# Five places for weight blocks and longer runs of paired slabs in a streamed MLP layer

## The chip, the cores and the metric

The kernel runs on one core of a Trainium2 chip. The metric is the device time of one execution in microseconds, the median of several runs. The profile comes from a single further execution, so its own time stands beside the median below.

## The reference

One encoder layer on a sequence of 256 tokens of width 2048, all in float32. Three residual branches follow one another: a mix of four token mixers, a cross attention, and a gated MLP; a norm ends it. The change touches the MLP and what feeds its weights.

```python
def swiglu(h, w_gate_up, w_down):
    gate, up = jnp.split(h @ w_gate_up, 2, axis=-1)
    return (jax.nn.silu(gate) * up) @ w_down
...
        x = x + mix @ w_out[l]
        x = x + cross_attention(rms_norm(x, norm_g[l, 1]), mem_n, w_xq[l], w_xkv[l], w_xo[l])
        x = x + swiglu(rms_norm(x, norm_g[l, 2]), w_gate_up[l], w_down[l])
    return rms_norm(x, final_norm_g)
```

w_gate_up is 2048 x 11264, w_down 5632 x 2048.

## The kernel before

**Arithmetic.** TensorE multiplies in a shorter format, fp32r. So each weight is used as a sum of two: `wh`, the weight cast to fp32r by ScalarE, and `wl`, the raw weight minus `wh`, subtracted by VectorE. Activations are kept in the same way as a high and a low half of one slot. `part` (L430) multiplies one activation tile of 128 tokens with 512 columns of weights in three matmuls: high x wh (L432), high x wl (L433), low x wh (L434).

**The stream of weights.** All weights of the layer come in one sequence of 252 slabs of 128 partitions x 2048 floats (16 blocks of 128 x 128). `Stream` (L72) loads and converts them. `_load` (L94) brings a slab into `raw` (three buffers) by a transfer on SP's queue. `_half` (L112) converts half a slab, 1024 columns: a cast at L135 and a subtraction at L136, into a *place*, a pair of tiles wh and wl. `_buffers` (L88) picks the place: three in the pool `wp`, and one in `extra`, a pool that exists in most of the kernel and takes every fourth block. `_fill` (L166) runs when TensorE's program takes a block: it writes down conversions until three blocks more than the one in use are made. So a block is converted into a place that TensorE has finished with, and the number of places sets how far the conversion runs ahead.

**Normal and paired slabs.** In w_gate_up and w_down a plan of letters says how each slab is used. In an N slab two halves of 1024 columns are multiplied with two tiles of 128 tokens: eight parts. In an S slab (`PAIRED`, L50) two tiles along the summed dimension, two groups of columns and the two tiles of tokens are multiplied as 2 x 2 blocks with seven products instead of eight (the Strassen-Winograd scheme). This needs sums of weight blocks, made from the raw slab, and sums of activations, made once by `combine` (L437) into tiles `z`. `_sums` (L140) hands out an S slab as four blocks of 1024, 512, 1024 and 1024 columns: two, one, two and two parts. Call s0, s1, s2 the first three quarters of the raw slab and s3 the last.

- block one (`ph` 0): s1 and s2 as loaded
- block two: s0 as loaded
- two adds on VectorE (L158): the tile `two` holds (s1 + s3, s2 + s3); the first add makes s1 := (s1 + s3) + s2, the second s2 := s1 + s0
- block three: `two`
- block four: s1 and s2, so it reads what the second add wrote

In w_gate_up (`SUMMED`, L52) the tile `two` is made by transfers: when the slab before an S slab is loaded, SP loads the last quarter of the S slab twice, into both halves of `two` (L101), and a transfer on POOL's queue adds the two middle quarters to it in memory (L102). The S slab's own raw load then brings three quarters only. `two` has two buffers of its own.

**The order of work.** The tile framework places the instructions of each engine at build time; `keep_place` (L308) pins a run of them behind the instruction before. Work that isn't part of the stream (norms, combinations, splitting of loaded activations) is written as generators in `Background` (L204), which is polled after each part and steps a generator when VectorE's counted backlog is under 0.9 us.

**The MLP.** Slabs 120 to 127 are the first columns of w_gate_up, by `gemm_rows` (L521); in this time the last features of the attention arrive (`ar`) and are put into the slots `h3`. Ten groups of eight slabs follow, slabs 128 to 207, by `paired_rows` (L463): each makes 512 gate and 512 up columns by the plan `GROUP`, "NNSNSNSN". In a group `mixed` (L1064) combines four of the seven products when the last S slab is done, and `gated` (L1073) applies the gate's nonlinearity after that when the gate's normal tiles are done, which by this plan is at the end of the last S slab (one N slab follows). `upped` and `up` multiply gate and up at the end of the group, and `store_turned` transposes the result and writes it to memory ("hidden"). `fetch` (L1087) loads it back and splits it into the slots `f` for w_down. The residual `res` (four tiles of 128 x 1024 floats) isn't used from the end of the attention until w_down. In w_down (slabs 208 to 251) the plans `PASSES` apply.

Of the kernel before, what the change touches and what calls it, by code (L numbers as in the profile page):

```python
# [13 lines left out]
F32 = mybir.dt.float32  # L14
F32R = mybir.dt.float32r
# [4 lines left out]
ALU = mybir.AluOpType  # L20
# [3 lines left out]
P = 128  # L24
# [25 lines left out]
PAIRED = {a + i for a, plan in [(GATE_UP + 8 * j, GROUP) for j in range(10)] + [(DOWN, PASSES[0]), (DOWN + 22, PASSES[1])]  # L50
          for i, x in enumerate(plan) if x == "S"}
SUMMED = {i for i in PAIRED if i < DOWN}  # L52

# [18 lines left out]
class Stream:  # L72


    def __init__(self, tc, pools, W, bg):
        self.tc, self.nc, self.W, self.bg = tc, tc.nc, W, bg
        self.rawp, self.wp = pools
        self.order = []
        self.n = self.made = 0
        self.after = []  # L80
        self.halves = []
        self.at = self.phase = 0
        self.raw = None
        self.extra = self.sums = None
        self.places = []
        self.two = []

    def _buffers(self, n, m):  # L88
# [165 lines left out]
class Block:  # L254
    def __init__(self, ctx, tc, t):
# [10 lines left out]
        self.st = Stream(tc, (rawp, wp), t["W"], self.bg)  # L266
        self.kept = itertools.count()
        self.run()

# [193 lines left out]
    def paired_rows(self, w, cols, slots, sums, plan, mixed, first, ready=None, late=0, before=None, swap=False):  # L463
# [23 lines left out]
        for i, kind in enumerate(plan):  # L487
            if before:
                before(i)
            if kind == "S":  # L490
                ks, z = next(todo)
# [75 lines left out]
    def run(self):  # L567
# [20 lines left out]
        self.ff = self.outside("hidden", FT)  # L588
        self.gk = [nc.dram_tensor(f"state{i}", (R, P), F32, kind="Internal").ap() for i in range(4)]
        self.vd = nc.dram_tensor("values", (P, 8 * 512), F32, kind="Internal").ap()  # L590
        def load(src, k, n):
# [16 lines left out]
        nc.scalar.copy(self.identr, self.ident)  # L608
        with self.tc.tile_pool(name="wx", bufs=1) as st.extra:
            self.attention(self.mixers())  # L610
# [256 lines left out]
    def attention(self, ps):  # L867
        tc, nc, act, st = self.tc, self.nc, self.act, self.st
        with tc.tile_pool(name="atp", bufs=1) as atp, tc.tile_pool(name="kp", bufs=1) as kp, \
# [110 lines left out]
            late.append(self.bg.add(self.arrive(self.xf[1], 2, self.tmp, self.put3, FAR), go=True))  # L980
            st.extra = None
            self.add_rows(1, 3, self.gemm_rows("w_xo", [1536], o)[0])
# [46 lines left out]
    def mlp(self):  # L1029
        tc, nc, act = self.tc, self.nc, self.act  # L1030
        with tc.tile_pool(name="fp", bufs=1) as fp:
            self.gap(fp, 192)
            f = [fp.tile([P, 512], F32R, name=f"f{i}") for i in range(14)]
            z = [fp.tile([P, 1024], F32R, name=f"z{i}") for i in range(3)]
            f = act[4:12] + f + [z[i // 2][:, i % 2 * 512:i % 2 * 512 + 512] for i in range(6)] + self.h3
            with tc.tile_pool(name="wy", bufs=1) as self.st.extra:
                self.gap(self.st.extra, 64)
                with tc.tile_pool(name="tw", bufs=2) as self.st.sums, tc.tile_pool(name="gp", bufs=1) as gp:
# [8 lines left out]
    def gate_up(self, gp, f, z):  # L1047
# [76 lines left out]
        comb = self.bg.add(combined())  # L1124
        ps = self.gemm_rows("w_gate_up", [0, DFF], self.h3,
                            parts=[(range(8), [0]), (range(8, 12), [0]), (range(12), [1]), (range(12, 16), [0]), (range(12, 16), [1])],
                            before=lambda n: n in (1, 3) and self.bg.drain(self.late if n == 1 else last))
        self.bg.drain(col)
# [4 lines left out]
        for j in range(1, DFF // 512):  # L1133
            upped(j, self.paired_rows("w_gate_up", [j * 512, DFF + j * 512], self.h3, sums, GROUP, mixed, gated, swap=j % 2 == 0)[0])
        self.bg.drain(early)
        self.fetch = self.bg.add(fetch(FT - 22, FT, 6, SOON))

    def down(self, f, sp):
# [54 lines left out]
        for i, plan in enumerate(PASSES):  # L1193
# [5 lines left out]
            def before(j):  # L1199
                while plan[j] == "S" and len(made) <= plan[:j].count("S"):  # L1200
                    self.bg.step(next(e for e in self.bg.q if e[0] is g))
                if late and j == len(plan) - 2:
                    st.extra = None

# [686 lines left out]
```

## Time and profile before

| what | us |
|---|---|
| median of three runs | 1437.49 (1437.12 to 1438.29) |
| the profiled execution's own time | 1434.72 |
| its span in the profile | 1432.9 |
| TensorE busy in it | 1423.0 |
| VectorE busy | 1145.7 |
| ScalarE busy | 815.8 |

Some 1.8 us of the profiled execution lie outside the span. Times in the views count from the span's start. A busy share is an average over the whole kernel; what a change in one part is worth is read from that part's own window. Matmuls overlap each other, so a matmul's own duration is longer than the pitch at which they follow one another. In the views L432 is line 432 of the kernel, `wl<-raw,wh` names the tiles written and read, and the name in brackets behind an idle time is what ended it.

### The profile page before, as it was taken

To read this page: it belongs to the slowest core of one execution; us is meant where nothing else is said; L and a number is where in the kernel's file an instruction comes from. 1 tells how busy PE (TensorE), PEld (TensorE's weight loads), DVE (VectorE), ACT (ScalarE), POOL (GpSimd) and SP (SyncE) were. 2 spreads that over 40 slices of the span, in tenths; PEclk is the share of its full clock that TensorE was granted. 3 is DMA by queue.
4 is the path that set the end of the run, shared out by engine and by line. 5 is a ranking of instruction groups with operands and counts; after the bars stand their busy time and mean duration, and the time that the engine had idled before them with its cause. 6 is when DMAs were issued, how large, how long until landed. Compare 5 with 4: busy or idle time off the path is not lost.

```text
span 1432.9 us, 18653 instructions
## 1 busy us (share of the span) xinstructions
PE 1423.0 (99%) x6589; PEld 1181.4 (82%) x6589; DVE 1145.7 (80%) x1738; ACT 815.8 (57%) x1183; POOL 234.6 (16%) x306
## 2 busy tenths in 40 slices
PE   9999999999999999999999999999999999999997
PEld 8888888888888888888888888888888888788886
DVE  6667868777877767777677888889888888989997
ACT  7556565446745555556455556555555556655655
POOL 0000100013212223531430121122011002000000
PEclk9999999999999999999999999999999999999999
DMA  9877554456667787865986989899999887665554
GB/s 350 299 291 247 205 202 166 171 172 224 198 199 232 235 271 246 275 201 171 287 242 207 283 280 289 275 275 285 294 293 289 264 265 227 217 231 180 193 219 147
DMA packets 73038, 343.80 MB, mean 240 GB/s; under 512 B 10957, under 2 KB 12654, under 8 KB 45168
## 3 DMA queue, kind: packets, MB, share of 16 engines
q1 hardware_dynamic: 54848, 288.98, 57.6%
q0 software_dynamic: 17664, 52.97, 15.6%
q8 instruction: 51, 0.84, 0.2%
q10 hardware_dynamic: 432, 0.66, 0.1%
q14 instruction: 43, 0.35, 0.1%
HBM read 322.12 MB, written 20.45 MB: 239 GB/s over the span
## 4 chain that ended last, share of the span: by engine, by line
PE 98%; DVE 1%; DMA 0%; ACT 0%; issue 0%; SPq 0%; ACTq 0%
PE pg L432 22%; PE pg L433 22%; PE pg L434 22%; PE pm L432 7%; PE pm L434 7%; PE pm L433 7%; PE pg L380 4%; PE pg L381 2%; PE pm L1344 1%; PE pm L1022 1%; PE pm L993 1%; PE pm L1753 0%; DMA raw<-in_W 0%; DVE res L282 0%; PE pm L994 0%; PE pm L1518 0%
## 5 line engine op out<-in xcount | busy, mean ns | idle before, releaser
L136 DVE TENSOR_TENSOR wl<-raw,wh 128x1024 fp32r<-128x1024 f32 (+1 forms) x413 | 494.1, 1211 | 167.6 <-ACT wh L135 164.8
L135 ACT CAST wh<-raw 128x1024 fp32r<-128x1024 f32 (+1 forms) x413 | 424.7, 1043 | 282.9 <-PE pg L434 188.3
L432 PE MATMUL pg<-wh,act 128*128 128x512 f32 (+1 forms) x1191 | 465.5, 391 | 0.0
L433 PE MATMUL pg<-wl,act 128*128 128x512 f32 (+1 forms) x1191 | 463.9, 389 | 0.1
L434 PE MATMUL pg<-wh,act 128*128 128x512 f32 (+1 forms) x1191 | 463.8, 390 | 0.0
L432 PEld LDWEIGHTS pg<-wh,act 128*128 128x128 f32 x1191 | 224.0, 188 | 47.9 <-issue 1.5
L434 PEld LDWEIGHTS pg<-wh,act 128*128 128x128 f32 x1191 | 223.9, 188 | 47.5 <-DVE act L282 0.6
L433 PEld LDWEIGHTS pg<-wl,act 128*128 128x128 f32 x1191 | 224.0, 188 | 46.5 <-DVE wl L136 1.2
L147 ACT CAST wh<-raw 128x1024 fp32r<-128x1024 f32 (+1 forms) x150 | 137.4, 921 | 149.6 <-PE pg L434 53.8
L148 DVE TENSOR_TENSOR wl<-raw,wh 128x1024 fp32r<-128x1024 f32 (+1 forms) x150 | 155.9, 1060 | 52.8 <-ACT wh L147 52.6
L433 PE MATMUL pm<-wl,act 128*128 128x512 f32 x309 | 120.3, 389 | 0.1
L432 PE MATMUL pm<-wh,act 128*128 128x512 f32 x309 | 120.2, 389 | 0.0
L434 PE MATMUL pm<-wh,act 128*128 128x512 f32 x309 | 120.2, 389 | 0.0
L380 PE MATMUL pg<-act,wh 128*128 128x512 f32 x256 | 90.5, 395 | 0.0
L381 PE MATMUL pg<-act,wl 128*128 128x256 f32 x256 | 71.8, 280 | 0.0
L433 PEld LDWEIGHTS pm<-wl,act 128*128 128x128 f32 x309 | 58.0, 188 | 12.3 <-DVE wl L136 0.4
L434 PEld LDWEIGHTS pm<-wh,act 128*128 128x128 f32 x309 | 58.0, 188 | 12.1
L432 PEld LDWEIGHTS pm<-wh,act 128*128 128x128 f32 x309 | 58.0, 188 | 12.0
L102 POOL DMA_DIRECT2D two<-in_W x30 | 26.6, 885 | 237.6 <-DMA two<-in_W 106.4
L158 DVE TENSOR_TENSOR raw<-raw 128x512 f32<-128x512 f32 x90 | 61.8, 687 | 1.2
L147 ACT CAST wh<-two 128x1024 fp32r<-128x1024 f32 x30 | 31.5, 1051 | 52.0 <-PE pg L434 27.0
L380 PEld LDWEIGHTS pg<-act,wh 128*128 128x128 f32 x256 | 48.1, 188 | 10.5
(375 smaller groups left out, 1819.3 us busy)
## 6 DMA issues: line engine op xcount, KB each, us to landing
raw<-in_W SPq DMA_DIRECT2D x216, 1024.0 KB, 5.6
raw<-in_W SPq DMA_DIRECT2D x30, 768.0 KB, 6.3
two<-in_W SPq DMA_DIRECT2D x60, 256.0 KB, 4.8
two<-in_W POOLq DMA_DIRECT2D x30, 512.0 KB, 9.0
raw<-in_W SPq DMA_DIRECT2D x11, 512.0 KB, 7.1
hidden<-g POOLq DMA_DIRECT2D x22, 256.0 KB, 3.8
tmp<-hidden POOLq DMA_DIRECT2D x44, 128.0 KB, 6.0
features<-tmp POOLq DMA_DIRECT2D x32, 128.0 KB, 5.2
```

The lines of the kernel that those rows point to most:

```text
L102: nc.gpsimd.dma_start(t, W[:, 512:1536], accum_op=ALU.add)
L135: nc.scalar.copy(wh[:, a:b], r[:, a:b])
L136: nc.vector.tensor_tensor(out=wl[:, a:b], in0=r[:, a:b], in1=wh[:, a:b].bitcast(F32), op=ALU.subtract)
L147: nc.scalar.copy(wh, src)
L148: nc.vector.tensor_tensor(out=wl, in0=src, in1=wh.bitcast(F32), op=ALU.subtract)
L158: nc.vector.tensor_tensor(out=out, in0=a, in1=b, op=ALU.add)
L380: self.nc.tensor.matmul(p[:, :], wh, slot[:, :], start=start, stop=False)
L381: self.nc.tensor.matmul(p[:, 0:R], wl, slot[:, 0:R], start=False, stop=stop)
L432: self.nc.tensor.matmul(p, hi, wh, start=start, stop=False)
L433: self.nc.tensor.matmul(p, hi, wl, start=False, stop=False)
L434: self.nc.tensor.matmul(p, lo, wh, start=False, stop=stop)
L993: nc.tensor.matmul(p[:, :], q[d][:, r * P:(r + 1) * P], kt[d][:, :], start=d == 0, stop=False)
```

## The change

It has four parts.

1. *The plans.* `GROUP` becomes two plans, used by turns: "NNSSSSNN" for the first, third and each other odd group, "NNSNSSNN" for the even ones. The ten groups hold 35 S slabs instead of 30. The last S slab is followed by two N slabs in both, so `mixed` and `gated` come one slab earlier in a group. A fourth `z` is needed: it takes the place of two of the slots `f` (14 of their own become 12), two more slots of `f` lie in the four `z`, and `fetch` holds back slots 20 and 21 until the last group, whose three S slabs leave `z[0]` free. The background makes four combinations of activations in the first eight slabs instead of three.
2. *The places.* The pools of places are kept in a list; the next block goes to the place that was written longest ago. `lend` adds a place, `back` takes it away. A fifth place, `wz`, is lent two slabs into the first w_gate_up product (`before(1)`) and given back in the last group.
3. *The memory of `two`.* The residual is written to memory at `before(1)` in four transfers of 512 KB on SP's queue, its four tiles serve as `two` by turns, and four transfers load it back after the ten groups.
4. *How `two` is filled.* SP loads the last quarter once, into the first half of `two`, four slabs ahead of the S slab. One slab later ScalarE copies it to the second half, pinned in its order, and POOL's queue adds the middle quarters.

The conversions, `part`, the adds and the w_down plans stay as they are.

```diff
-GROUP = "NNSNSNSN"
+GROUPS = "NNSSSSNN", "NNSNSSNN"
...
+AHEAD = (-4, -3)
+
+SUMS = [{GATE_UP + 8 * j + i + a: GATE_UP + 8 * j + i for j in range(10) for i, x in enumerate(GROUPS[j % len(GROUPS)]) if x == "S"}
+        for a in AHEAD]
...
-        self.extra = self.sums = None
+        self.ring = [[self.wp, -1] for _ in range(3)]
+        self.sums = []
...
-        pool = self.extra if self.extra and len(self.halves) % 4 == 3 else self.wp
+        slot = min(self.ring, key=lambda x: x[1])
+        assert slot[1] < self.at or slot[1] < 0
+        pool, slot[1] = slot[0], len(self.halves)
...
-        if n // 16 + 1 in SUMMED:
-            W, t = self.W[n // 16 + 1], self.sums.tile([P, 1024], F32, name="two", tag="two")
-            for a in (0, 512):
-                nc.sync.dma_start(t[:, a:a + 512], W[:, 1536:2048])
-            nc.gpsimd.dma_start(t, W[:, 512:1536], accum_op=ALU.add)
+        if n // 16 in SUMS[0]:
+            t = self.sums[0]
+            self.sums.append(self.sums.pop(0))
+            nc.sync.dma_start(t[:, 0:512], self.W[SUMS[0][n // 16]][:, 1536:2048])
+            self.begun.append(t)
+        if n // 16 in SUMS[1]:
+            t = self.begun.pop(0)
+            mark = len(nc.cur_bb.bb.instructions)
+            nc.scalar.copy(t[:, 512:1024], t[:, 0:512])
+            self.keep(mark)
+            nc.gpsimd.dma_start(t, self.W[SUMS[1][n // 16]][:, 512:1536], accum_op=ALU.add)
             self.two.append(t)
...
-        ahead = self.at + 1 + min(3 if self.extra else 2, self.n // 16)
+        ahead = self.at + 1 + min(len(self.ring) - 1, self.n // 16)
...
+    def lend(self, pool):
+        self.ring.append([pool, -1])
+        return pool
+
+    def back(self, pool):
+        self.ring = [x for x in self.ring if x[0] is not pool]
...
-            f = [fp.tile([P, 512], F32R, name=f"f{i}") for i in range(14)]
-            z = [fp.tile([P, 1024], F32R, name=f"z{i}") for i in range(3)]
-            f = act[4:12] + f + [z[i // 2][:, i % 2 * 512:i % 2 * 512 + 512] for i in range(6)] + self.h3
+            f = [fp.tile([P, 512], F32R, name=f"f{i}") for i in range(12)]
+            z = [fp.tile([P, 1024], F32R, name=f"z{i}") for i in range(4)]
+            f = act[4:12] + f + [z[i // 2][:, i % 2 * 512:i % 2 * 512 + 512] for i in range(8)] + self.h3
...
+                    while k0 == 0 and k - ahead >= 20 and "free" not in box:
+                        yield
...
-        sums = [((2 * i, 2 * i + 1), z[i]) for i in range(GROUP.count("S"))]
+        sums = [((2 * i, 2 * i + 1), z[(i + 1) % 4]) for i in range(4)]
...
+        def before(n):
+            if n == 1:
+                self.st.lend(self.wz)
+                for c, x in enumerate(whole):
+                    nc.sync.dma_start(self.rd[:, c * 1024:(c + 1) * 1024], x)
+                self.st.sums = list(whole)
+            if n in (1, 3):
+                self.bg.drain(self.late if n == 1 else last)
...
+            plan = GROUPS[(j - 1) % len(GROUPS)]
+            if j == 10:
+                box["free"] = True
+            upped(j, self.paired_rows("w_gate_up", [j * 512, DFF + j * 512], self.h3, sums[:8 - plan.count("N")], plan, mixed, gated,
+                                      before=lambda i: (j, i) == (10, 5) and self.st.back(self.wz), swap=j % 2 == 0)[0])
+        for c, x in enumerate(whole):
+            nc.sync.dma_start(x, self.rd[:, c * 1024:(c + 1) * 1024])
```

More of the change, by code (lines that the diff above doesn't have):

```diff
@@ L267, in __init__ @@
         self.kept = itertools.count()
+        self.st.keep = self.keep_place
         self.run()
@@ L489, in paired_rows @@
                 before(i)
[L490 removed]
+            if kind in "Ss":
                 ks, z = next(todo)
@@ L589, in run @@
         self.gk = [nc.dram_tensor(f"state{i}", (R, P), F32, kind="Internal").ap() for i in range(4)]
+        self.rd = nc.dram_tensor("residual", (P, 4 * 1024), F32, kind="Internal").ap()
         self.vd = nc.dram_tensor("values", (P, 8 * 512), F32, kind="Internal").ap()
@@ L608, in run @@
         nc.scalar.copy(self.identr, self.ident)
-        with self.tc.tile_pool(name="wx", bufs=1) as st.extra:
+        with self.tc.tile_pool(name="wx", bufs=1) as self.wx:
+            st.lend(self.wx)
             self.attention(self.mixers())
@@ L980, in attention @@
             late.append(self.bg.add(self.arrive(self.xf[1], 2, self.tmp, self.put3, FAR), go=True))
-            st.extra = None
+            st.back(self.wx)
             self.add_rows(1, 3, self.gemm_rows("w_xo", [1536], o)[0])
@@ L1121, in combined @@
                 yield from self.combine(z, *(self.h3[k] for k in ks))
-        sums = [((2 * i, 2 * i + 1), z[i]) for i in range(GROUP.count("S"))]
+        sums = [((2 * i, 2 * i + 1), z[(i + 1) % 4]) for i in range(4)]
         comb = self.bg.add(combined())
+        whole = [x.rearrange("p k r -> p (k r)") for x in self.res]
+        def before(n):
[6 more added lines that the diff above has]
+                self.bg.drain(self.late if n == 1 else last)
         ps = self.gemm_rows("w_gate_up", [0, DFF], self.h3,
                             parts=[(range(8), [0]), (range(8, 12), [0]), (range(12), [1]), (range(12, 16), [0]), (range(12, 16), [1])],
-                            before=lambda n: n in (1, 3) and self.bg.drain(self.late if n == 1 else last))
+                            before=before)
         self.bg.drain(col)
@@ L1202, in before @@
                 if late and j == len(plan) - 2:
-                    st.extra = None
+                    st.back(self.wy)
             ps, rest = self.paired_rows("w_down", [2 * i * 512, (2 * i + 1) * 512], f, sums[:n], plan,
```

15 lines of the change are left out of this document (8 added, 7 removed).

## The prediction

> **What bounds the kernel now.** I read the page's busy line and its chain of waits first, then the groups, and then the windows of the stretch in which the paired slabs of w_gate_up run.
>
> ```profile
> span 1432.9 us, 18653 instructions
> PE 1423.0 (99%) x6589; PEld 1181.4 (82%) x6589; DVE 1145.7 (80%) x1738; ACT 815.8 (57%) x1183; POOL 234.6 (16%) x306
> PE 98%; DVE 1%; DMA 0%; ACT 0%; issue 0%; SPq 0%; ACTq 0%
> L432 PE MATMUL pg<-wh,act 128*128 128x512 f32 (+1 forms) x1191 | 465.5, 391 | 0.0
> 789.00:1204.00 415.00, 415.00 (x1832) 343.67 (x1832) 359.74 (x424) 236.67 (x275) 65.05 (x76) 1.00 0.90 278
> ```
>
> TensorE is busy for 1423.0 of 1432.9 us, and the chain of what ended last runs through it for 98%. The last row is a window (start and end, length, then busy us and instructions of PE, PEld, DVE, ACT, POOL, then clock, DMA share, GB/s) over the ten groups of eight slabs: PE was busy in all 415.00 us, at a granted clock of 1.00. So nothing feeds TensorE late there, and this stretch gets shorter only by fewer matmuls and longer only by a wait that isn't there now. Matmuls overlap, so their 391 ns are no price: 415.00 / 1832 = 0.2265 us is the pitch, and a part (three matmuls) costs 0.68 us. A normal slab (N, eight parts) lasts 5.44 us, a paired one (S, seven parts) 4.76.
>
> **What is removed on TensorE.** The groups have three S each, 30 in all. The new plans alternate four and three, five groups of each: 35. Five slabs lose one part each, so 15 matmuls go: 15 x 0.2265 = **-3.40 us**. No other matmul changes, so this is the most that the edit can gain while the clock row stays at 1.00.
>
> **What is added: VectorE's work comes in bursts.** Every weight block has to be subtracted on VectorE before its second matmul, and an S slab also needs two adds. The prices are in the timeline of VectorE around two S slabs of one group (start, duration, instruction, idle before it):
>
> ```profile
> 912.38 1.22 DVE L148 TENSOR_TENSOR wl<-two,wh 128x1024 fp32r<-128x1024 f32 x1
> 913.52 0.68 DVE L158 TENSOR_TENSOR raw<-raw 128x512 f32<-128x512 f32 x1
> 914.12 0.41 DVE L282 TENSOR_TENSOR f<-tmp,f 128x256 fp32r<-128x256 f32 x1
> 915.39 1.23 DVE L148 TENSOR_TENSOR wl<-raw,wh 128x1024 fp32r<-128x1024 f32 x1 [0.86 <-ACT wh L147]
> 916.53 2.35 DVE L136 TENSOR_TENSOR wl<-raw,wh 128x1024 fp32r<-128x1024 f32 x2
> 918.80 1.82 DVE L148 TENSOR_TENSOR wl<-raw,wh 128x1024 fp32r<-128x1024 f32 x2
> 920.54 0.68 DVE L158 TENSOR_TENSOR raw<-two,raw 128x512 f32<-128x512 f32 x1
> 921.26 0.69 DVE L158 TENSOR_TENSOR raw<-raw 128x512 f32<-128x512 f32 x1
> ...
> 924.85 1.23 DVE L148 TENSOR_TENSOR wl<-raw,wh 128x1024 fp32r<-128x1024 f32 x1 [1.09 <-ACT wh L147]
> ```
>
> The two full subtractions at 916.53 are followed by the next at 918.80, so one costs (918.80 - 916.53) / 2 = 1.14 us of VectorE. The row at 918.80 is a full and a half one, followed at 920.54: 1.74 - 1.14 = 0.60 for the half. The first add costs 921.26 - 920.54 = 0.72 with its dependent behind it, and 0.60 otherwise (913.52 to 914.12). An S slab is three full, one half, two adds: 3 x 1.14 + 0.60 + 2 x 0.60 = 5.22 us, or 5.34 with the dependent add. TensorE uses it up in 4.76. **So VectorE falls behind by 0.46 to 0.58 us in each S slab**, and gains 5.44 - 2.28 = 3.16 in each N slab. Before, an N slab follows every S slab, and this never adds up. Now four S come in a row in five groups. In the other five plans S stands alone once and twice in a row once.
>
> How much can it fall behind? That is the spare time of a block, and the places set it. The fourth block of an S slab is the tight one:
>
> ```profile
> 926.92 0.39 PE L432 MATMUL pg<-wh,z 128*128 128x512 f32 x1
> 927.15 0.39 PE L433 MATMUL pg<-wl,z 128*128 128x512 f32 x1
> 908.14 0.62 ACT L147 CAST wh<-raw 128x512 fp32r<-128x512 f32 x1 [1.16 <-PE pm L434]
> 914.31 1.05 ACT L147 CAST wh<-raw 128x1024 fp32r<-128x1024 f32 x1 [2.11 <-DVE raw L158]
> 923.77 1.05 ACT L147 CAST wh<-raw 128x1024 fp32r<-128x1024 f32 x1 [1.41 <-DVE f L282]
> ```
>
> Its subtraction ends at 924.85 + 1.23 = 926.08, and the matmul that reads it starts at 927.15: 1.07 us to spare. The working: with four places, its place is free when TensorE has used the block four earlier; between lie three blocks, five parts, 3.40 us, and cast, wait and subtraction take 1.08 (923.77 to 924.85) + 1.23, with some 0.2 to start. 3.40 + 0.23 (the second matmul is the one that waits) - 2.5 = 1.1, as measured. **With five places** four blocks lie between, a whole slab: 4.76 + 0.23 - 2.5 = **2.5 us**. That is the edit's own answer to the bursts, and 3 x 0.58 = 1.7 fits into it. If each slab's operations stayed together there would be no stall.
>
> But order on VectorE is fixed at build time, and in the rows it isn't always the slab's own. The fourth block reads the second add's result. At 913.52 that add runs behind the third block, and the fourth has to wait for a cast on top: 914.31 - (913.52 + 0.68) = 0.11, and 1.08 from the cast's start to the subtraction's, 1.19 in all, of which 0.86 shows as idle. A fifth place lets the following slab's first blocks (1.14, and 0.60 for the half) be converted at this point instead, as nothing but a free place holds them back. Then the fourth block is put off by 1.14 + 0.60 = 1.74. Through a run of four: spare 2.5 - 1.74 = 0.76 at the first S, 0.76 - 0.57 = 0.19 at the second, -0.38 at the third, -0.95 at the fourth. **TensorE waits 0.95 us per run, 5 x 0.95 = 4.8 us.** Groups with two in a row stay above zero.
>
> Bounds of this cost: none at all, where both adds precede the third block as they did at 920.54 and 921.26 (0 us); and, where the cast is waited for idly in every slab, 3 x (0.46 + 1.19) - 2.5 = 2.4 per run, 12 us. I take 4.8, between them, because both orders stand side by side in the rows above and a fifth place favours the late one. A gain beyond -3.40 is excluded: PE has no idle time left to recover.
>
> Beside the row at 918.80 (two operations, 1.82 us, the next at 920.54, 0.08 before their end), the Trainium skill, "VectorE: DVE Perf Modes", section "The DRAIN you can't avoid", says that an operation doesn't start until the pipe of the one before is empty, so that a sequence costs the sum of its durations. By it an S slab would be 3 x 1.23 + 3 x 0.68 = 5.7 us by estimate, and a run would stall for about 1.1 us more; these rows disagree with it, if only slightly.
>
> **The other edits.** Their prices and covers:
>
> ```profile
> raw<-in_W SPq DMA_DIRECT2D x216, 1024.0 KB, 5.6
> raw<-in_W SPq DMA_DIRECT2D x30, 768.0 KB, 6.3
> two<-in_W SPq DMA_DIRECT2D x60, 256.0 KB, 4.8
> two<-in_W POOLq DMA_DIRECT2D x30, 512.0 KB, 9.0
> res<-in_xT SPq DMA_DIRECT2D x4, 512.0 KB, 6.6
> 736.00:778.00 42.00, 42.00 (x187) 34.77 (x186) 30.59 (x65) 23.80 (x36) 6.37 (x8) 1.00 0.72 230
> ACT act L294 <- DMA ar<-features: 3.7, 1, 3.7
> ```
>
> *The fourth block's copy.* One 256 KB load fewer per S; ScalarE copies 128x512 instead (0.62 us, the row at 908.14), 35 x 0.62 = 22 us onto 236.67 of 415. It doesn't wait for TensorE, but casts queue behind it if the load is late; it is issued a slab after the load, 4.8 to 5.4 us against 4.8 to landing. Covered; bare, a wait of up to 0.6 each on the cast, inside the lead of 2.5. The accumulating transfer now starts three slabs ahead (14.3 us or more) against 9.0.
>
> *Residual out and in.* Four stores and four loads of 512 KB on SP's queue. The stores are issued in the first group of w_gate_up, where the DMA share is 0.72, and can delay the features (waited for 3.7 us there) and the raw loads behind them; PE is 42.00 of 42.00 busy there. By the row of 6.6 us for such transfers and the raw lead of at least one slab, 5.44, I take 0 and bound it by 6.6 - 5.44 = 1.2. The loads are needed only in w_down, well over 30 us later. SP has no compute queued behind them, only raw loads.
>
> *One more combination of activations* in the first eight slabs: some twelve VectorE operations of 0.2 to 0.4 us, about 3 us on 30.59 of 42: covered by 11 us idle; bare, 3 us. *Two tiles of the hidden layer split late* (0.41 each, row 914.12) and *the mixing of a group's sums moved ahead of the last two N slabs* instead of one: its VectorE work then meets 2 x 3.16 of surplus: 0, or a small gain in the spare that counts for nothing here.
>
> **The sum.** -3.40 + 4.8 = +1.4 us on the profiled execution, whose span of 1432.9 and 1.8 around it make 1434.7: 1436.1. The median of the three timed runs is 1437.49, 2.8 above the profiled one, so I forecast 1437.5 + 1.4 = **1439** (case A). Its own range is 1436.5 to 1442: stalls of half to one and a half times 4.8.
>
> **The rivals.**
>
> *B, the bursts are fully carried.* The spare of 2.5 holds 3 x 0.58 = 1.7, the adds stay ahead of the third block, and only -3.40 remains: 1434.1. For it speaks the order at 920.54; against it the order at 913.52. *B', a little waits:* 0.3 us per run, -1.9: 1435.6.
>
> *C, slower: raw weights land late in the run of four.*
>
> ```profile
> ACT wh L135 <- DMA raw<-in_W: 32.0, 10, 4.2
> ACT wh L147 <- DVE raw L158: 17.9, 9, 2.3
> ```
>
> The first row (total, times, longest) shows ScalarE waiting for raw loads ten times in the ten groups, 3.2 us each, now hidden by the places. An S slab draws 768 + 256 + 512 KB = 1.57 MB in 4.76 us, 330 GB/s; the window above moved 278 at a DMA share of 0.90, so the ceiling is about 309. In 4 x 4.76 = 19 us some 0.4 MB falls short, 1.3 us. Three raw buffers absorb that if they are full, but a run also starts behind VectorE's lag. If each of the five runs meets one such wait of 3.2 with only the 0.76 of spare left, it pays 5 x (3.2 - 0.76) = 12 us: -3.4 + 12 = +8.8, **1446**. It decides from a wait of 0.76 us upward. Against it: over a group the bytes fall, because each S loads 256 KB less from the second tile.
>
> *D, the change doesn't do what it says:* if places were lent out of turn so that only four serve the run, the spare is 1.07 and 3 x 0.57 is more than that by 0.64 even without reordering: 5 x 0.64 = 3.2, about 1437.3, inside A and B'.
>
> **How the numbers follow.** A and D 0.40, B 0.28, B' 0.10, C 0.22. The range reaches from B with a little below it for the runs' own spread (1433.7) to C (1446). What a measurement of this kernel can tell from no change is 0.2%, 2.9 us: faster than 1434.6 is most of B, 0.27; A splits, most of it and B' within, 0.35; slower than 1440.4 is C and the upper part of A, 0.38.
>
> **What would show it right or wrong.** Right: PE x6574, and PE idle in the five groups of four, in their third and fourth S, released by the fourth block's subtraction on VectorE, with subtractions of the next slab's first block ahead of it on VectorE. B: windows over the groups with PE busy in every microsecond, 3.4 us shorter. C: casts that wait for raw loads, with PE idle right behind them. Wrong altogether: a span shorter by more than 3.4, PE idle in the first eight slabs beside the residual's stores, or idle in w_down from late residual.

## The result: 1453.85 us, 1.2% slower

The median of four runs is 1453.85 us (1452.1 to 1456.5) against 1437.3 for the kernel before (four runs, 1436.11 to 1438.29). The ratio is 1.0117 (95% interval 1.0100 to 1.0135): some 17 us slower, and outside the predicted range of 1433.7 to 1446.

The page of the profiled execution afterwards, and the same two stretches of both kernels in the windows view: from the 3400th matmul, which is near 700 us in both, to the start of the ten groups, and the ten groups themselves (start and end, length, then busy us and instructions of PE, PEld, DVE, ACT, POOL, then clock, DMA share, GB/s). First the kernel after:

```profile
span 1452.0 us, 18599 instructions
PE 1430.4 (99%) x6574; PEld 1177.0 (81%) x6574; DVE 1160.7 (80%) x1766; ACT 834.5 (57%) x1230; POOL 238.7 (16%) x311
PE 23%; DVE 6%; issue 2%; DMA 2%; ACT 2%; POOL 0%; ACTq 0%; DVEq 0%; POOLq 0%
701.03:785.47 84.44, 81.28 (x346) 66.53 (x345) 54.55 (x101) 43.97 (x68) 21.36 (x27) 0.96 0.86 265
785.47:1212.39 426.92, 419.70 (x1817) 338.05 (x1816) 372.84 (x446) 253.90 (x315) 69.53 (x81) 1.00 0.87 262
```

and the kernel before:

```profile
699.97:777.94 77.97, 77.97 (x345) 64.56 (x344) 53.83 (x95) 43.02 (x63) 21.20 (x26) 1.00 0.79 247
777.94:1192.80 414.86, 414.86 (x1831) 343.57 (x1830) 356.88 (x420) 234.82 (x271) 67.80 (x79) 1.00 0.90 277
```

The 15 matmuls are gone (6574 instead of 6589). Before, 1830 matmuls of the groups took 414.86 us, 0.2267 each, with TensorE never idle. At this pitch the 1815 of after need 411.46; they took 426.92. So the groups **lose 15.5 us** beside the 3.4 gained. The stretch ahead of them **loses 6.5 us** (84.44 - 77.97), in which the mean granted clock fell to 0.96. The first 47 us differ by 1.0 from run to run, w_down by 0.1: 15.5 + 6.5 + 1.0 - 3.4 - 0.1 = 19.5, and the 0.4 by which the two profiled spans differ less (19.1) lies behind the last matmul. The busy share is 99% in both: a late matmul has a longer duration in the rows (0.50 and more instead of 0.39), so most of its wait counts as busy. The length of a stretch against its number of matmuls shows the loss.

**Ahead of the groups.** TensorE's rows around the first loss, then SP's queue and ScalarE in the same time (start, duration, engine and line, name, and the idle time with what ended it):

```profile
735.26 0.39 PE L457 MATMUL pg<-wh,act 128*128 128x512 f32 x1
737.86 0.50 PE L455 MATMUL pg<-wh,act 128*128 128x512 f32 x1 [2.21 <-ACT wh L150]
739.31 0.80 PE L456 MATMUL pg<-wl,act 128*128 128x512 f32 x1 [0.94 <-DVE wl L151]
...
740.32 0.63 PE L455 MATMUL pg<-wh,act 128*128 128x512 f32 x1
740.75 0.63 PE L456 MATMUL pg<-wl,act 128*128 128x512 f32 x1
```

```profile
715.52 0.33 SPq L1159 DMA_DIRECT2D residual<-res  x1
722.30 0.33 SPq L110 DMA_DIRECT2D res<-in_W  x1
723.03 17.71 SPq L123 DMA_DIRECT2D raw<-in_W  x4
...
SPq L110 <- DMA residual<-res: 8.4, 2, 6.4
...
735.81 2.94 ACT L150 CAST wh<-raw 128x1024 fp32r<-128x1024 f32 x3 [7.24 <-DMA raw<-in_W]
```

A store of the residual is issued at 715.52, when its data are there. The next entry of the queue, a load of a fourth block into the same tile (L110), needs that store to have landed and waits 6.4 us. The scheduler had moved it ahead of raw loads that are needed sooner. The first of these goes out at 723.03, though the subtraction that frees its buffer had ended at 719.01; the next two (724.48 and 729.86) leave when their buffers come free. Now these loads, the load of L110 and the features' transfers run together: the load of 724.48 lands after 11.3 us, at 735.79, where its counterpart before took 5.1.

ScalarE's next cast reads that second slab. In the order fixed at build time it stands ahead of the casts of the slab before it, whose data had landed at 730.55. The kernel before had the two in the same order, and it cost 1.00 us of ScalarE and nothing of TensorE:

```profile
728.51 2.00 ACT L135 CAST wh<-raw 128x1024 fp32r<-128x1024 f32 x2 [1.00 <-DMA raw<-in_W]
```

In the change ScalarE idles 7.24 us there, and the cast that TensorE needs runs second in the row at 735.81. TensorE waits 2.4 + 1.2 us more than a pitch, and afterwards its matmuls come 0.43 us apart instead of 0.23: the clock was granted at half for 6.8 us.

**In the groups.** Loss by slab against its number of matmuls (worked out from the matmuls' starts), for two groups of each plan:

```
group 5  NNSSSSNN   0    0    0   1.65 0.57 0.42 0.04 0    2.7 us
group 7  NNSSSSNN   0    0    0   1.15 0.25 1.39 0.08 0    2.9
group 4  NNSNSSNN   0    0    0    0    0   0.73  0   0    0.7
group 6  NNSNSSNN   0    0   0.42 0.13  0   0.84 0.02 0    1.4
```

The five groups with a run of four lose 12.1 in all (1.06 of it at the very first slab, which waits for the gate's activation), the others 3.4. The rows of VectorE and ScalarE in the run of group 5 (`wl<-res` is a third block, since `two` lies in the residual's tiles now):

```profile
973.15 1.22 DVE L163 TENSOR_TENSOR wl<-res,wh 128x1024 fp32r<-128x1024 f32 x1
974.29 0.68 DVE L173 TENSOR_TENSOR raw<-raw 128x512 f32<-128x512 f32 x1
976.16 2.96 DVE L163 TENSOR_TENSOR wl<-raw,wh 128x1024 fp32r<-128x1024 f32 x3 [1.19 <-ACT wh L162]
...
975.09 2.51 ACT L162 CAST wh<-raw 128x1024 fp32r<-128x1024 f32 x3 [3.05 <-DVE raw L173]
...
977.45 0.50 PE L456 MATMUL pm<-wl,z 128*128 128x512 f32 x1 [0.76 <-DVE wl L163]
```

The third block's subtraction (973.15) stands ahead of the second add (974.29). ScalarE, idle for 3.05 us, casts the fourth block only behind the add; VectorE idles 1.19 us for that cast, and TensorE waits for the subtraction.

By the order of casts and subtractions in the trace, the third block stands ahead of the second add in 32 of the 35 paired slabs. In 19 of the 35 no other conversion stands between that add and the fourth block, so VectorE waits for the cast or splits activations meanwhile. In 14, 12 of them in the runs of four, a later block's subtraction stands there, ahead of the fourth. The last paired slab of the same run is one of these: the next N slab's block at 988.68 comes before the fourth block at 989.88.

```profile
988.08 0.69 DVE L173 TENSOR_TENSOR raw<-raw 128x512 f32<-128x512 f32 x1
988.68 1.22 DVE L151 TENSOR_TENSOR wl<-raw,wh 128x1024 fp32r<-128x1024 f32 x1
989.88 1.23 DVE L163 TENSOR_TENSOR wl<-raw,wh 128x1024 fp32r<-128x1024 f32 x1
```

### The profile page after: what moved, and what is told of

Same layout as the page of the kernel before. It is cut to its first block, busy times and chain, and to the rows that moved or that the text cites. A ratio compares the mean times of both kernels' runs of the same rounds, so it can differ in the third digit from the quotient of the medians.

```text
span 1452.0 us, 18599 instructions
## 1 busy us (share of the span) xinstructions
PE 1430.4 (99%) x6574; PEld 1177.0 (81%) x6574; DVE 1160.7 (80%) x1766; ACT 834.5 (57%) x1230; POOL 238.7 (16%) x311
## 5 line engine op out<-in xcount | busy, mean ns | idle before, releaser
L455 PE MATMUL pg<-wh,act 128*128 128x512 f32 (+1 forms) x1161 | 454.5, 393 | 4.0 <-ACT wh L150 3.2
L456 PE MATMUL pg<-wl,act 128*128 128x512 f32 (+1 forms) x1161 | 454.1, 391 | 2.1 <-DVE wl L151 1.9
L457 PE MATMUL pg<-wh,act 128*128 128x512 f32 (+1 forms) x1161 | 453.5, 391 | 0.2 <-DVE act L305 0.2
L455 PEld LDWEIGHTS pg<-wh,act 128*128 128x128 f32 x1161 | 218.4, 188 | 52.4 <-ACT wh L150 5.3
L456 PEld LDWEIGHTS pg<-wl,act 128*128 128x128 f32 x1161 | 218.8, 188 | 49.3 <-DVE wl L151 4.8
L457 PEld LDWEIGHTS pg<-wh,act 128*128 128x128 f32 x1161 | 218.7, 188 | 47.1 <-DVE act L305 1.3
L455 PE MATMUL pm<-wh,act 128*128 128x512 f32 x314 | 122.4, 390 | 0.0
L457 PE MATMUL pm<-wh,act 128*128 128x512 f32 x314 | 122.3, 390 | 0.0
L117 POOL DMA_DIRECT2D res<-in_W x35 | 30.9, 884 | 267.7 <-ACT res L115 256.7
L457 PEld LDWEIGHTS pm<-wh,act 128*128 128x128 f32 x314 | 59.0, 188 | 12.1
L173 DVE TENSOR_TENSOR raw<-raw 128x512 f32<-128x512 f32 x95 | 65.2, 686 | 0.7
L587 POOL DMA_DIRECT2D tmp<-hidden x44 | 38.8, 888 | 73.4 <-issue 38.2
```

Source lines behind the costliest of these rows:

```text
L117: nc.gpsimd.dma_start(t, self.W[SUMS[1][n // 16]][:, 512:1536], accum_op=ALU.add)
L173: nc.vector.tensor_tensor(out=out, in0=a, in1=b, op=ALU.add)
L455: self.nc.tensor.matmul(p, hi, wh, start=start, stop=False)
L456: self.nc.tensor.matmul(p, hi, wl, start=False, stop=False)
L457: self.nc.tensor.matmul(p, lo, wh, start=False, stop=stop)
L587: self.nc.gpsimd.dma_start(t.rearrange("p (g t) -> p g t", t=32), src)
```

## The experiments

Each edit is against the changed kernel, and the line numbers are the same. The table gives the loss of the two stretches as above (length less 77.97; length less 0.2267 a matmul), the median and the ratio to the kernel before on the same chip. The losses are those of one profiled execution, whose own time lies up to 3.3 us from the median, and 6.1 above it in pairs_four.

| kernel | lost ahead | lost in groups | median | ratio (95%) |
|---|---|---|---|---|
| the change | 6.5 | 15.5 | 1453.85 | 1.0117 (1.0100 to 1.0135) |
| pin_adds | 5.9 | 8.7 | 1443.22 | 1.0043 (1.0029 to 1.0058) |
| pin_sp | 6.7 | 19.6 | 1456.63 | 1.0140 (1.0125 to 1.0155) |
| both_pins | 7.0 | 5.9 | 1443.75 | 1.0045 (1.0030 to 1.0061) |
| old_plan | 6.5 | 14.6 | 1454.86 | 1.0129 (1.0112 to 1.0146) |
| no_store | 0.0 | 17.2 | 1448.17 | 1.0079 (1.0060 to 1.0098) |
| old_plan_pin | 5.6 | 5.9 | 1447.98 | 1.0079 (1.0055 to 1.0103) |
| old_plan_four | 6.5 | -0.1 | 1440.20 | 1.0027 (1.0018 to 1.0037) |
| four_places | 5.2 | 7.7 | 1443.75 | 1.0051 (1.0035 to 1.0067) |
| new_four | 5.3 | 17.5 | 1454.08 | 1.0118 (1.0101 to 1.0135) |
| spread | 0.0 | 8.1 | 1438.42 | 1.0017 (1.0006 to 1.0028) |
| pairs | 0.0 | 15.1 | 1446.19 | 1.0066 (1.0049 to 1.0082) |
| pairs_four | 5.9 | 26.3 | 1457.78 | 1.0155 (1.0128 to 1.0182) |
| between | 0.0 | 7.9 | 1439.27 | 1.0016 (1.0006 to 1.0027) |
| lead | 1.3 | 6.4 | 1437.68 | 1.0009 (0.9996 to 1.0023) |
| nine | 0.5 | 14.9 | 1455.30 | 1.0126 (1.0106 to 1.0146) |
| old_four_spread | 1.3 | 2.7 | 1437.38 | 0.9998 (0.9985 to 1.0011) |
| two_and_two | 2.3 | 3.3 | 1434.94 | 0.9992 (0.9984 to 1.0000) |
| two_and_two_four | 1.5 | 30.8 | 1465.81 | 1.0198 (1.0184 to 1.0212) |

**pin_adds: the second add ahead of the third block.** `behind` sets an order alone, without a wait.

```diff
-        self.bg.dve(src.shape[1])
+        self.bg.dve(src.shape[1]); ph == 2 and summed and self.behind(self.added)
...
+            self.bg.dve(512 * len(ops), len(ops)); self.added = nc.cur_bb.bb.instructions[-1].name
```

> The changed kernel with one order fixed: on VectorE the third block's subtraction stands behind the second add. Theory 1 (idle waits): the 14.2 us lost in the ten groups come from the second add standing behind the third block's subtraction, so that ScalarE's cast of the fourth block starts late and VectorE idles 0.9 to 1.2 us per paired slab; with the add first, at most 2 us remain: 1440 to 1444. Theory 2 (bursts): VectorE's work of 5.3 us per 4.76 us overflows the lead of the places by itself; still 10 us or more in the groups, 1450 to 1455. Theory 3 (late raw weights): nothing moves, 1452 to 1456.

1443.22 us, inside theory 1's range, but more than its 2 us remain in the groups. They lost 8.7, of which 4.1 at the very first slab (the gate again, this time with the clock at half behind it); the even groups but the last lost nothing, and the runs of four 0.3 to 1.6 each. Late raw weights are out as the cause of what went: ScalarE waited for raw loads 51.6 us in the groups here, and 45.1 in the change. The order takes away the idle wait for the cast and most of the overtaking (4 of the 35 fourth blocks still have a later block ahead), so this run doesn't tell what each of the two cost.

**pin_sp: SP's queue in program order**, for L110 and the residual's stores, by `keep_place`; and **both_pins**, with the adds fixed too.

> The changed kernel with the residual's four stores and the loads of the fourth blocks kept on SP's queue in the order in which they are written in the program. Theory 1 (a queue held up): the stores that wait for the residual and the early loads that wait for the stores hold back raw loads behind them; with the order kept, the 3.95 us wait near 737 us and the 2.6 us of lowered clock behind it go: 1446 to 1449, the groups unchanged. Theory 2 (bytes): the stores' 2 MB delay the raw loads wherever they stand, 1452 to 1456.

> Both orders fixed. If the idle waits and the held queue are the causes, the gains add up: 1433 to 1437.5, and the groups run without a gap in TensorE of more than 2 us in all. If bursts overflow the lead: 1443 to 1449.

1456.63 and 1443.75, against both first theories: the order on SP's queue cures nothing. The loss ahead of the groups is there again (6.7), in another place. ScalarE's row in pin_sp:

```profile
756.08 0.51 ACT L317 ACTIVATE act<-ar,vec 128x256 fp32r<-128x256 f32 x1 [7.44 <-DMA ar<-features]
...
758.13 1.99 ACT L150 CAST wh<-raw 128x1024 fp32r<-128x1024 f32 x2
759.22 0.49 PE L455 MATMUL pg<-wh,act 128*128 128x512 f32 x1 [2.55 <-ACT wh L150]
```

Now the four stores ran at 735 to 738, just as the features go out to memory and back. The features came late, ScalarE waited 7.44 us for them (3.7 before), and the casts stood behind that wait in its queue, ready but out of turn. (In the change ScalarE waited 7.0 us for the same features, until 761.56, and no matmul came late for it.)

**old_plan: NNSNSNSN in all groups**, all else as changed (`GROUPS = "NNSNSNSN",`).

> The changed kernel with the plan of before, NNSNSNSN in all groups (30 paired slabs), and all else as changed: five places, residual's memory, the copy by ScalarE. If the runs of paired slabs are needed for the loss in the groups, these lose nothing and only the 6.5 us near 737 us stay: 1443 to 1446. If the places, the copy or the transfers cost time by themselves: 1449 or more.

1454.86 us: without any run of paired slabs the groups lost 14.6 us, most of it in the first S slab of groups 3 to 8 and 10. So something else in the change can cost as much by itself.

**no_store: no store of the residual and no load back.**

> The changed kernel without the residual's four stores to memory and four loads back (the last sum then starts from what the tiles hold after the groups, so the output is not the reference's). Theory 1 (traffic): the 2 MB written between 690 and 760 us delay the features' way through memory and the raw loads, and ScalarE's casts queue behind what waits for them; without the stores the 6.4 us lost ahead of the groups go, groups as before: 1446 to 1449. Theory 2 (not the stores, but the fourth combination or the fifth place lent there): 1452 to 1456.

1448.17 us, theory 1 for the stretch ahead: 0.0 lost. The groups lost 17.2 (4.2 of it at the very first slab).

**old_plan_pin and old_plan_four**: the old plan with the add's order fixed, and the old plan without the fifth place (`lend(self.wz)` left out, nothing else).

> The plan of before with all else as changed, and the third block's subtraction fixed behind the second add. The plan alone was no cure: it lost 14.5 us in the groups, at the first paired slab of a group. Theory 1 (order of the add): the 1.2 us that VectorE waits there for a cast falls away; the groups lose 3 us or less: 1441 to 1445. Theory 2 (the fifth place: conversions run up against raw loads that have not landed, and the group's mixing queues behind them on VectorE, 2.0 us late): at least 6 us stay in the groups, 1446 to 1452.

> The plan of before with all else as changed but without the fifth place. Theory 1 (order of the add, fifth place harmless): nothing is better with a place less, 12 us or more lost in the groups, 1453 to 1460. Theory 2 (the fifth place is what lets conversions run up against raw loads): the groups run as before, at most 2 us lost: 1440 to 1446.

1447.98 and 1440.20 us. Without the fifth place the groups ran without a gap (414.80 us for 1830 matmuls); with it, and the adds in order, they still lost 5.9. The late mixing of theory 2 is seen in VectorE's rows around the start of the fifth group (954.30 in old_plan, 951.19 in old_plan_four). First old_plan:

```profile
948.42 3.50 DVE L151 TENSOR_TENSOR wl<-raw,wh 128x1024 fp32r<-128x1024 f32 x3 [0.20 <-ACT wh L150]
951.84 0.68 DVE L305 TENSOR_TENSOR h<-g,pg 128x512 f32<-128x512 f32 x1
954.92 1.23 DVE L151 TENSOR_TENSOR wl<-raw,wh 128x1024 fp32r<-128x1024 f32 x1 [2.40 <-ACT wh L150]
956.06 0.68 DVE L305 TENSOR_TENSOR g<-h,pg 128x512 f32<-128x512 f32 x1
...
963.93 1.78 DVE L163 TENSOR_TENSOR wl<-raw,wh 128x1024 fp32r<-128x1024 f32 x2
```

and old_plan_four:

```profile
947.79 0.68 DVE L305 TENSOR_TENSOR g<-h,pg 128x512 f32<-128x512 f32 x1
...
957.90 1.82 DVE L163 TENSOR_TENSOR wl<-raw,wh 128x1024 fp32r<-128x1024 f32 x2
```

With five places three subtractions stand in a row ahead of the group's mixing (h<-g,pg, g<-h,pg; with four places it is two), and a fourth in its middle waits 2.40 us for its cast. The mixing's second add runs 1.8 us behind the group's start instead of 3.4 ahead of it, and the first S slab's blocks come at 9.6 us of the group instead of 6.7. A place more lets conversions stand earlier in the order; they use up VectorE's turn, not idle time.

**four_places and new_four**: the new plans without the fifth place, with the adds fixed and without.

> The new plans with the second add fixed ahead of the third block, but without the fifth place. Theory 1 (the fifth place carries the bursts): the spare of 1.07 us holds one paired slab's excess and not three, 3 to 8 us more than with five places (1443.2): 1446 to 1451. Theory 2 (the fifth place does harm): 1437 to 1442.

> The change without the fifth place, and nothing else altered (no order fixed). Theory 1 (the fifth place does the harm, by letting subtractions of later slabs stand ahead of the group's mixing and of the second add): the groups lose 8 us or less instead of 15.4: 1443 to 1448. Theory 2 (the runs of paired slabs do the harm, and a place less makes it worse): 15 us or more, 1453 to 1460.

1443.75 and 1454.08 us. The first lies between its two theories; for new_four theory 2 holds: without the fifth place the new plans lose as much (17.5 against 15.5). Between these two kernels the order of the add alone differs, and it is worth 9.8 us in the groups. The rows of new_four show its price:

```profile
974.05 2.96 DVE L163 TENSOR_TENSOR wl<-raw,wh 128x1024 fp32r<-128x1024 f32 x3 [1.19 <-ACT wh L162]
...
980.54 2.96 DVE L163 TENSOR_TENSOR wl<-raw,wh 128x1024 fp32r<-128x1024 f32 x3 [1.19 <-ACT wh L162]
```

One paired slab to the next takes VectorE 980.54 - 974.05 = 6.49 us against TensorE's 4.76, and the last two paired slabs in groups 1, 5 and 9 lost 1.7 us each.

With the add first, four places lost 7.7: 0.2 to 0.6 us in each group of NNSNSSNN and 0.9 to 1.5 in each run of four. Five lost 4.6 besides the 4.1 at the gate. So with order kept the fifth place saved some 3 us in these profiles, but the medians of the two kernels are the same (1443.75 and 1443.22). Neither kernel with four places lost anything at the gate; in the change the gate's activation stands on ScalarE behind a cast that waits 4.75 us for its raw load. And with the old plan the fifth place costs time even with order kept (5.9 in old_plan_pin, nothing in old_plan_four).

**spread: stores one by one.** The adds fixed; one store ahead of each of the raw loads of slabs 122, 123, 126, 127; L110 in order.

```diff
+AHEAD = (-4, -3); STORES = {122: 0, 123: 1, 126: 2, 127: 3}
...
+        ...; n // 16 in STORES and self.store(STORES[n // 16])
```

> The changed kernel with the second add fixed ahead of the third block, and the residual's stores moved: one each ahead of the raw loads of slabs 122, 123, 126 and 127 on SP's queue, in fixed order, as are the loads of the fourth blocks. Theory 1 (the stores cost by when they run and by what waits behind them): the 6.5 us ahead of the groups go, the groups as with both orders fixed (4.5 to 6): 1436 to 1440. Theory 2 (the bytes cost wherever they stand): 1442 to 1446.

1438.42 us, theory 1 for the stretch ahead: nothing is lost there, with the same 2 MB moved. (The later kernels with spread stores lost 0 to 2.3 there, and pairs_four 5.9, in a profiled execution 6.1 above its median, so placing them isn't a sure cure.) The groups lost 8.1, more than the 4.5 to 6 expected, 1.4 of it at the first slab, for the gate:

```profile
699.82:777.79 77.97, 77.97 (x345) 64.56 (x344) 54.36 (x101) 43.86 (x67) 20.89 (x26) 1.00 0.93 280
777.79:1197.31 419.52, 415.07 (x1816) 339.71 (x1815) 374.42 (x445) 254.83 (x315) 69.46 (x81) 1.00 0.88 268
```

In the groups the runs of four are what is left, and VectorE's rows in one of them show no idle time for a cast as long as 1.19 any more:

```profile
1047.55 1.22 DVE L163 TENSOR_TENSOR wl<-res,wh 128x1024 fp32r<-128x1024 f32 x1
1048.82 2.96 DVE L163 TENSOR_TENSOR wl<-raw,wh 128x1024 fp32r<-128x1024 f32 x3
1051.70 0.68 DVE L173 TENSOR_TENSOR raw<-res,raw 128x512 f32<-128x512 f32 x1
...
1054.30 2.96 DVE L163 TENSOR_TENSOR wl<-raw,wh 128x1024 fp32r<-128x1024 f32 x3
```

5.48 us from slab to slab against 4.76: 0.72 per slab, and the slabs behind the point where the lead is gone lose 0.71 to 0.74 each.

**pairs and pairs_four**: spread with NSSNSSNN for the four, with five places and with four.

> As spread, but the plan with four paired slabs is NSSNSSNN, so that at most two stand in a row. If the rest of the loss in the groups is the run of four (0.57 us per slab against a spare of 2.5): at most 1.5 us in the groups, 1433 to 1436.5. If it is something else (the mixing meets the first paired slab's banks, raw loads late): 1438 to 1442.

> As pairs, without the fifth place. A pair's excess of 0.57 us fits in the spare of 1.07 with four places: 1433 to 1437, as with five. If the fifth place carries more than that, 1438 to 1442.

Both expectations failed: 1446.19 and 1457.78. The loss sits in the first paired slab (1.9 to 4.2 and 2.9 to 6.2 us): it stands in the second place of the group, where VectorE still has the group before to mix. In group 7 of pairs the last steps of the mixing and the transposes (1037.16 to 1040.30) stand ahead of the third block's subtraction, for which TensorE waits 2.78 us. Not the run's length alone counts, but also what it meets.

**between, lead, nine**: the adds between the subtractions; no background work in paired slabs; four paired slabs in nine groups.

> As spread, with two differences: the first add stands between the first and the second block's subtraction and the second behind the second (so that no add follows the one that it depends on), and the residual's stores stand earlier (ahead of slabs 119, 121, 123 and 127). Theory (throughput): with the pins VectorE needs 5.48 us for a paired slab in a run, of which 0.12 is the dependent add and 0.14 the wait for a cast; both go, and a run of four loses at most 0.5 us instead of 1.6: groups 2 to 4 us instead of 8.0, 1432.5 to 1436. Rival (the rest is late raw weights or background splits): 1437 to 1440.

> As between, and the background (splits of loaded hidden tiles, 0.41 us of VectorE each) is not called on in paired slabs of w_gate_up, only in normal ones. If splits inside the runs are what is left: the groups lose 1.5 us or less, 1432 to 1435. If not: as between.

> As lead, with four paired slabs in nine groups and three in the last: 39 paired slabs instead of 35, 12 matmuls (2.7 us) fewer. If runs of four cost 0.3 us or less each by then: 1430 to 1433.5. If two such groups behind one another leave VectorE no time to catch up (39 us of work in 40.8): 1435 or more.

1439.27, 1437.68, 1455.30. The times of the rivals came out. The adds' new places gained nothing: the slabs behind the point where the lead is gone still lost 0.65 to 0.75 us each, and in lead VectorE's rows are again 5.48 us apart from slab to slab (1130.06 to 1135.54). Without background work the runs of four lost 0.3 to 1.8 us each, 5.0 together, more than the 5 x 0.68 that their additional slabs save. nine lost 0.7 to 1.9 in each of nine runs, and some 11 us more at the start of w_down, where the clock was at half; that part wasn't followed up.

**old_four_spread**: the old plan, four places, the residual's memory and the copy, stores placed.

> The plan of before, four places, no pinned adds; the residual's memory, the copy by ScalarE and the stores placed as in between. Theory (these parts cost nothing once the stores and loads are placed): as before within 0.2%, 1434 to 1437.5. Rival (the copy and the additional transfers have a price of their own): 1439 or more.

1437.38 us against 1436.78: no difference, by the interval of the ratio to within 0.15%. The memory and ScalarE's copy cost nothing that can be told from this, once the stores are placed; the profiled execution lost 1.3 ahead and 2.7 in the last group.

**two_and_two and two_and_two_four**: lead with NNSSNSSN by turns with NNSNSSNN; and four places, by turns with NNSNSNSN.

> As lead (five places, adds between, stores placed, no background inside paired slabs), but the plan with four paired slabs is NNSSNSSN: two pairs, the first in the third place as before. If 0.72 us per paired slab against a lead of 2.5 is the whole account, a pair costs nothing: groups at most 1.5 us, 1432.5 to 1435.5, below before. If the mixing, which now comes one slab later in these groups, queues behind subtractions as in the kernel with the old plan: 1437 to 1441.

> Four places, NNSSNSSN by turns with NNSNSNSN, adds between, stores placed. With four places the mixing ran on time and lone paired slabs lost nothing; a pair lost 0.25 to 0.35 us (four_places, the sixth slab of the even groups), so ten pairs lose some 3 us and the gain of 3.4 is all but used up: 1435 to 1438. If the first pair meets the mixing as well: 1440 or more.

two_and_two ran in 1434.94 us, 1.4 below before (1436.38); the interval of its ratio ends at 1.0000, so a gain is not shown clear of noise. Eight of its ten groups lost nothing, two lost 1.6 to 1.7 at the first S slab behind a cast that waited for its raw load, and 2.3 was lost ahead of the groups, in a profiled execution that was 3.3 us above the median. two_and_two_four lost 30.8: the second slab of each group behind an NNSSNSSN waited 3.6 to 7 us. Its expectation was far off. In group 4 the cast of the first paired slab (918.10) waits 4.13 us for its raw load, the gate's activation stands behind it on ScalarE, VectorE waits 3.69 us for that, and the subtraction that TensorE needs (921.70) stands behind. Why four places do so much worse here wasn't tried.

## Why the prediction was wrong

**The gain on TensorE** (-3.40) held: 15 matmuls fewer at the pitch worked out.

**"I take 0 and bound it by 1.2"** for the residual's stores failed; they cost 6.5 (no_store, spread). The prediction weighed the transfers' bytes and length against one raw load's lead. It did not ask what the stores and the loads into the same tiles wait for, nor what stands behind them in a queue: a load that waits 6.4 us for a store held a raw load 4 us, and a cast out of slab order waited for the transfers that then ran together. It quoted the row by which ScalarE waits 3.7 us for the features, but did not follow that one either: in pin_sp and both_pins the casts stood behind a longer wait for them. Behind the first 2 us of waiting came the halved clock, which the sum lacked: 13 matmuls x 0.2 = 2.6 us.

**The bursts** were mis-sized: 4.8 us forecast, 15.5 measured in the groups. The prediction took 0.95 us per run, from later blocks that overtake the fourth, and nothing elsewhere. The overtaking is there, in 14 of 35 paired slabs. But VectorE's idle wait for the fourth block's cast is there too, in place of it, and the prediction named that as the other bound only (0.46 + 1.19 = 1.65 us per slab, 12 in all). The runs of four lost 11.0, near this bound, and six slabs of new_four lost 1.7 each with that idle wait in their rows. Both come from the one order that it had read at 913.52, the second add behind the third block: fixing this order alone took away 6.8 us (9.8 without the wait at the gate), and 9.8 between new_four and four_places. How the loss divides between the two was not separated. "Groups with two in a row stay above zero" was wrong too: four of these five groups lost 0.5 to 1.4 us each, 3.4 together.

**"That is the edit's own answer to the bursts"** failed for the fifth place. The prediction reckoned a place as spare time, 2.5 us instead of 1.07. It did write that a place lets later blocks be converted first, but took that for a cost inside runs alone. old_plan and old_plan_four show that with the old plan it costs 14.6 us, by what it lets stand ahead of the mixing. With the new plans no such cost is shown: new_four, without the place, lost more than the change.

**Rival B** (the lead of 2.5 holds 3 x 0.58) did not hold even with every order fixed. A slab's excess was 0.72 instead of 0.58, as VectorE took 5.48 us for it where the prediction had 5.22 to 5.34; and 3 x 0.72 = 2.2 would still fit into 2.5, so the lead was not whole either. Background work takes a part of it (the runs lost 7.9 in between and 5.0 in lead); that the mixing takes the rest is argued from its place in the order, not shown. **Rival C** (late raw weights) had the right sign and half the size, for a reason that pin_adds speaks against: raw loads were waited for longer than before (45.1 us, 15 times, instead of 32.0, 10 times), but pin_adds waited longer still and lost half. They come in where a cast that waits holds up others, as at the gate and in two groups of two_and_two. **Rival D** is out: with four places the old plan lost nothing in the groups and with five 14.6, so the fifth was in use. The copy (old_four_spread) and the combination (no_store, 0.0 lost ahead) cost nothing that these runs show, as predicted.

**The sum of durations.** The section of the Trainium skill that the prediction sets beside its rows ("VectorE: DVE Perf Modes", "The DRAIN you can't avoid") adds that a next operation that is not held starts earlier. The rows agree with this addition: a subtraction lasts 1.22 us or more and the next starts 1.14 behind it.

## What to carry to other kernels

A further buffer is not only spare time: where order is fixed at build time, it can let later work stand ahead of what others wait for, and the engine's turn is spent. So fix the order of short dependent steps (here an add ahead of a cast on another engine) before adding buffers or runs. For a transfer that is "hidden", look up what shares its memory traffic on a round trip, and what is queued behind the one that waits for it.

## What was not expected of the hardware

A wait of TensorE of about 2 us costs more than itself. In the change the windows view gives 0.96 as the mean clock of the stretch with the wait of 2.4 us, and the trace's clock record half speed from 738.3 to 745.1. Over all 20 profiles, no wait of up to 1.8 us that stood alone (between 300 and 1400 us of the span) had a halved clock behind it, while all but two of 1.9 us or more (2.4 in pairs, 3.5 in two_and_two_four) had, for 3.4 or 6.8 us and once for 10.2. The Trainium skill, "TensorE: Matmul & The Clock Gate", section "Part 1: The HAM clock gate", has the clock halved after an idle window of about 3.4 us; the length of the slow time agrees with such windows, but waits of 1.9 to 2.4 us were enough here, in some kernels with a second of 1.0 to 1.2 right behind.
